# A two-layer conditioned decoder trunk on one Trainium2 core: another way through the opening, modulations on another engine, and a search over instruction orders

## The chip, the core and the metric

The kernel runs on one core of one Trainium2 chip. The core has five instruction streams that run side by side and meet only at semaphores: TensorE (PE: matmuls, transposes), VectorE (DVE), ScalarE (ACT), GpSimd (POOL) and SyncE (SP, which here issues nearly all DMA transfers). SBUF and PSUM are its on-chip memories; matmul results appear in PSUM and are read from there by DVE or ACT. The metric is the device time of one execution in microseconds (us), as the median of the runs; lower is better.

## The reference

Two layers over 256 tokens of width 1024 (batch 1). Each layer is a half-step SwiGLU FFN (width 2816), a token mixer, and another half-step FFN; layer 0 mixes with MoBA attention (16 heads of 64; with 256 tokens there is a single block, so it is causal attention with a relative bias), layer 1 with MLA attention on low-rank queries and a shared K/V. Every part starts with an RMS norm and a modulation whose shift, scale and gate come from the conditioning vector c:

```python
def rms_norm(x, g):
    return x * rsqrt(mean(x * x, -1) + EPS) * g
def modulate(h, shift, scale):
    return h * (1 + scale) + shift
def swiglu(h, w_gate, w_up, w_down):
    return (silu(h @ w_gate) * (h @ w_up)) @ w_down

c_act = silu(c)
for layer in range(2):
    mods = c_act @ ada_w[layer] + ada_b[layer]
    sh1, sc1, g1, sh2, sc2, g2, sh3, sc3, g3 = split(mods, 9)
    h = modulate(rms_norm(x, norm_g[layer, 0]), sh1, sc1)
    x = x + 0.5 * g1 * swiglu(h, ffn_w_gate[layer, 0], ffn_w_up[layer, 0], ffn_w_down[layer, 0])
    h = modulate(rms_norm(x, norm_g[layer, 1]), sh2, sc2)
    if layer == 0:
        mix = moba_attention(h, ...)
    else:
        k, v = mla_shared_kv(x, c_act, ...)   # own norm, shift and scale on x, then down and up projections
        mix = mla_attention(h, ..., k, v)
    x = x + g2 * mix
    h = modulate(rms_norm(x, norm_g[layer, 2]), sh3, sc3)
    x = x + 0.5 * g3 * swiglu(h, ffn_w_gate[layer, 1], ffn_w_up[layer, 1], ffn_w_down[layer, 1])
```

All data are float32.

## The kernel before

**Products.** A float32 product is made of three matmuls in the type fp32r: each operand is split into a rounded part "hi" and the rest "lo", and hi x hi, lo x hi and hi x lo are added in PSUM (`mm3`, lines 774 to 776). The split is made on the chip: ACT copies with rounding (`hi`, L644 for weights, L789 for activations), and DVE subtracts (`lo`, L645 and L790; `split_evac` is this pair for activations). Weights come from HBM through SP's queue into `raw` tiles, once each, as 128-row slabs of up to 1024 columns, and are used once.

**Conditioning.** The shift and scale columns of a norm (`m_cols`, one value for each of the 1024 features, laid out over partitions) are c_act times a slab of adaLN weights. `column` (L655) does 128 of them at a time: DVE multiplies a 128x1024 slab `adaw` (512 KB) with `c_b`, which holds c_act in every partition, and reduces. `scale_col` (L660) then turns the scale column s with the norm's gain g into (s + 1) g.

**Opening.** `first` (from L1518) serves the first FFN. c arrives as 32 rows of 256, is put through Silu (L1562, L1563), split (L1564), and eight matmuls (L1568) with a stationary operand `row_r` that selects one row broadcast it to all partitions; ACT copies the two PSUM tiles to `c_b` (L1571). Matmuls on zeros (L1579, "fills") keep PE at work and open the six accumulators `accs`. x is normed: the first row tile's square sum on DVE (L1589), the second's on ACT (L1586), `rstd` on POOL (L811), and a diagonal matrix with it (L1593) lets a matmul transpose and scale x at once (L1603); for later k a transpose is used (L1608). Then a loop over k = 0 to 7, one step for each 128 features: two `column` reduces, `scale_col`, the modulation `z` by ACT (L1620), its split into h (L789, L790), the split of the first FFN's weights for these features (`whi` by ACT, L1631; `wlo` by DVE, L1632; 768 KB a step, a 1024-column and a 512-column part, three 512-column parts at k = 0), and 36 matmuls (L1640 to L1642) into the six accumulators.

**Mixer entry.** After an FFN, `norm_T` norms a row tile (t = 0 or 1, 128 tokens) and `modulate_cols` (L816) treats it 256 columns at a time: ACT scales by rstd (L819), PE transposes (L824), and `modulate` (L836) applies scale and shift to each 128x128 block, by DVE (L840) or by ACT (L842), before the split. Before MLA this is done for two keys at once: the layer's own norm, (1, 1), into `h`, and the shared K/V's, "kv", into `hkv`. The line that selects the engine sends all of the second key to DVE, and of the first key the columns from 512 on. Behind it come the low-rank projections, whose results are normed and transposed into `qlT` and `ckT` (from L1397) and projected up.

**Order.** The kernel is first written down as one list of instructions. `Order` (L250) then chooses, for each of the five engines, the order in which its instructions are issued, by placing them one by one on a model of the chip with a cost for each (`duration`, L203) and a time by which it is needed (`needs`, L362); `place` (L377) does one placement, `work_out` (L517) repeats it four times with the PE times of the last one and keeps the best, and `apply` (L531) pins that order. Within an engine instructions run strictly in this order, and an instruction that waits holds up all behind it. `place` adds a cost when PE turns to plain float32 matmuls (`SWITCH`).

Of the kernel before, what the change touches and what calls it, by code (L numbers as in the profile page):

```python
# [4 lines left out]

# [16 lines left out]
P = 128  # L22
D = 1024
KD = D // P
S = 256
# [157 lines left out]

WAKE = 100.0
SWITCH = 95.0
COLD = 5600.0
TABLE = 1280.0
RATE = 330.0
# [4 lines left out]
MARGIN = 400.0  # L193
GATE_MARGIN = 3000.0
ROUND_OF_ORDER = 4
ENGINES = ("PE", "DVE", "Activation", "Pool", "SP")


# [4 lines left out]
def duration(i, aps):  # L203

    kind, e = type(i).__name__, i.engine.name
    n = max([elements(x) for x in aps] or [0])
    if kind == "InstDMACopy":
        return (700.0 if e == "Pool" else 330.0), 0.0
    if e == "PE":
        if kind != "InstMatmult":  # L210
            return 12.0, 12.0
        cols, dt = elements(aps[-1]), i.ins[0].dtype
        if i.is_transpose:
            c = 109.0
        elif dt == F32R:
            c = max(256, cols) / 2.4 + 13.3
        elif dt == F32:
            c = 2 * max(112.0, cols / 1.2 + 2.5)
            if DH in (aps[-1].ap[0][1], aps[0].ap[0][1]):
                c /= 2  # L220
        else:
            c = max(29.0, cols / 2.4 + 7.0)
        return c, c + 165.0
    psum = any(x.tensor.space == PSUM for x in aps)
    if e == "DVE":
        if kind == "InstTensorScalarPtr":
            full = len([x for x in aps if elements(x) == n]) > 2
            d = 205.0 + (1.05 if full else 0.54) * n if n > 8 else 155.0
            if aps[-1].tensor.dtype == mybir.dt.bfloat16 and n > 8:
                d = 267.0 + 0.42 * n  # L230
        elif kind == "InstTensorCopy":
            d = 150.0 + (1.045 if psum else 0.53) * n
        elif kind == "InstMemset":
            d = 60.0 + 0.84 * n
        else:
            d = 155.0 + 1.09 * n if kind in ("InstISA", "InstCustomDveAnt") else 150.0 + 1.045 * n
        return max(d - 83.0, 40.0), d
    if e == "Activation":
        d = (165.0 if psum else 195.0) + 0.845 * n + 95.0 * (len(aps) - 2) + 15.0 * (len(i.outs) > 1)
        return d - 110.0, d  # L240
    if e == "Pool":
        if kind == "InstTensorTensor":
            d = 600.0 + 300.0 * n if n <= 8 else 150.0 + 4.5 * n
        else:
            d = 60.0 + 0.9 * n if kind == "InstMemset" else 140.0 + 1.22 * n
        return d - 70.0, d
    return 50.0, 50.0


class Order:  # L250
# [4 lines left out]
    def __init__(self, nc, tc, rank, held, late, anchor):  # L255
# [34 lines left out]
        for name, us in self.uses.items():  # L290
            t = self.tiles[name]
            if t.space == DRAM:
                continue
            tag = str(t.tag).rsplit("_", 1)[0]
            pool = max((p for p in pools if tag.endswith("_" + p)), key=len)
            r = self.ring[name] = pool, tag
            if r not in self.bufs:
                self.bufs[r] = pools[pool].tag_meta[tag[:-len(pool) - 1]].bufs
            l = self.rings.setdefault(r, [])
            if l and self.uses[l[-1]][0] != us[0]:  # L300
                self.after[self.uses[l[-1]][0]].append(us[0])
                self.npre[us[0]] += 1
            if len(l) >= self.bufs[r]:
                self.next_tile[l[-self.bufs[r]]] = name
            l.append(name)
            for u in us:
                self.tiles_of[u].append(name)

    def add(self, i, seen, masks):
# [67 lines left out]
    def place(self, need):  # L377
# [68 lines left out]
        while placed < n:  # L446
# [68 lines left out]
        return order, max(done)  # L515

    def work_out(self):  # L517
        t, pe_time, best = 0.0, [0.0] * len(self.ins), None
        for k, e in enumerate(self.eng):
            if e == "PE":  # L520
                pe_time[k] = t
                t += self.cost[k][0]
        for _ in range(ROUND_OF_ORDER):
            order, end = self.place(self.needs(pe_time))
            if best is None or end < best[0]:
                best = end, order, self.start, self.done
            pe_time = self.start
        self.best = best
        return best

# [8 lines left out]
def trunk(ctx: ExitStack, tc: tile.TileContext, a: dict, out: bass.AP):  # L539
# [276 lines left out]
    def modulate_cols(t, r, keys, c0, n, wait):  # L816
# [4 lines left out]
        def fin():  # L821
            pt = tr_tile()[:, :n]
            for j in range(n // P):
                nc.tensor.transpose(kslice(pt, j), kslice(y, j), ident)  # L824
            pe(n // P * 0.11)
            for i, (key, h) in enumerate(keys):
                z = tp.tile([P, n], F32, tag="y", name=nm("z"), bufs=4) if i else y
                step = n if c0 or i else P
                for c in range(0, n, step):
                    modulate(pt[:, c:c + step], z[:, c:c + step], key, (c0 + c) // P, step,  # L830
                             on_vector=i > 0 or len(keys) > 1 and c0 >= 512)
                    split_h(h, c0 + c, step, z[:, c:c + step])
        due[0] = max(clock[0] + wait, due[0] + 0.01)
        later(due[0] - clock[0], fin)

    def modulate(xT, z, key, k0, n, on_vector=False):  # L836
        for j in range(n // P):
            shift, scale = [col_slice(i, key, k0 + j, 1) for i in range(2)]
            if on_vector:
                nc.vector.tensor_scalar(kslice(z, j), kslice(xT, j), scale, shift, op0=ALU.mult, op1=ALU.add)  # L840
            else:
                nc.scalar.activation(kslice(z, j), kslice(xT, j), AF.Identity,  # L842
                        scale=scale, bias=shift)

    def split_h(h, c0, n, z):
        ks = slice(c0 // P, (c0 + n) // P)
# [43 lines left out]
    def kslice(tile_, k):  # L890
        return tile_[:, k * P:(k + 1) * P]
# [626 lines left out]
    def first(units):  # L1518
# [5 lines left out]
        with ExitStack() as st:  # L1524
# [2 lines left out]
            with ranked(0):  # L1527
                nc.vector.memset(zeros, 0.0)

            c4, chi, clo = [tp.tile([P, S], x, tag="y", name=nm("c"), bufs=4)[:32] for x in (F32, F32R, F32R)]  # L1530
            row_r = fp.tile([32, 4], F32R, name="row_r")
            nc.vector.tensor_copy(row_r, ident[:32, :4])
            wt = [[splitp.tile([P, D], F32, tag=g, name=nm("adaw")) for g in ("hi", "lo")] for _ in range(KD)]
            cuts = (0, FIRST_A, n1)
            raws = [rawp.tile([P, 2048], F32, tag="raw", name=nm("raw")) for _ in range(3)]
# [10 lines left out]
                        nc.sync.dma_start(w[:, c1:c1 + step], src[:, c1:c1 + step])  # L1546

            with ranked(0):
                nc.scalar.dma_start(c4, a["c"])
                nc.scalar.dma_start(all_cols, a["cols"])  # L1550
            for t in range(NT):
                with ranked(t):
# [6 lines left out]
                    with ranked(2 * k + 3):  # L1559
                        load_w(k)  # L1560
            with ranked(0):
                nc.scalar.activation(chi, c4, AF.Silu)  # L1562
                nc.scalar.activation(c4, c4, AF.Silu)  # L1563
                nc.vector.tensor_tensor(clo, c4, chi.bitcast(F32), op=ALU.subtract)  # L1564
                pc = [tr_tile() for _ in range(2)]
                for x in (chi, clo):
                    for k in range(4):
                        nc.tensor.matmul(pc[k // 2][:, k % 2 * S:(k % 2 + 1) * S], row_r[:, k:k + 1].to_broadcast([32, P]), x,  # L1568
                                         start=x is chi and k % 2 == 0, stop=x is clo and k % 2 == 1)
                for i in range(2):  # L1570
                    nc.scalar.activation(c_b[:, i * 512:(i + 1) * 512], pc[i], AF.Copy)  # L1571
            hold(lambda: nc.scalar.activation(cact, cact, AF.Silu), 10e3)
            ps_x = [tr_tile(), ps_ada.tile([P, 512], F32, tag="ada", name=nm("tr"))]
            accs = [tr_tile() if f >= 4 else mm_tile() for f in range(B1)]


            for f in range(B1):
                for i in range(2 if 1 <= f < 4 else 1):
                    nc.tensor.matmul(accs[f], zeros, zeros[:, None].to_broadcast([P, 4, P]), start=i == 0, stop=False)  # L1579
            diag, rs, y, fill = [], [], {}, 10  # L1580
            for t in range(NT):
# [32 lines left out]
            for k in range(KD):  # L1614
                with ranked(2 * k + 2):
                    for i in range(2):
                        column(key, i, k, wt[k][i])
                    scale_col(key, k, 1)
                    z = tp.tile([P, S], F32, tag="y", name=nm("z"), bufs=4)
                    nc.scalar.activation(z, xT[k], AF.Identity, scale=col_slice(1, key, k, 1), bias=col_slice(0, key, k, 1))  # L1620
# [73 lines left out]
```

## Time and profile before

| | |
|---|---|
| median of 3 runs | 994.26 us (993.56 to 994.35) |
| the profiled execution: its own time | 993.19 us |
| the profiled execution: its span | 990.8 us |
| PE busy | 979.4 us, 5565 matmuls |
| DVE busy | 845.8 us |
| ACT busy | 629.2 us |
| POOL busy | 85.6 us |
| moved by DMA | 260.55 MB, 263 GB/s in the mean |

The span runs from the first to the last instruction of the profile; the execution's own time has a little more around it. The stages lie one behind the other: opening and first FFN to about 200 us, MoBA to about 330, two FFNs to 690, MLA's entry to 730, the rest of MLA to 830, the last FFN to the end.

A row of the timeline reads: start in us, duration in us, engine, line of the kernel, operation, what is written from what, shape, how many in a row; in brackets the time that the engine sat idle before it, and what released it. Rows with a count are several instructions merged, and their duration covers all of them. Neighbouring rows of one engine overlap a little, since an instruction's start lies ahead of the end of the one before. A row of the list of waits gives the waiting line and what it waited for, then the total in us, how many times, and the longest.

### The profile page before, as it was taken

To read this page: it belongs to the slowest core of one execution; us is meant where nothing else is said; L and a number is where in the kernel's file an instruction comes from. 1 tells how busy PE (TensorE), PEld (TensorE's weight loads), DVE (VectorE), ACT (ScalarE), POOL (GpSimd) and SP (SyncE) were. 2 spreads that over 40 slices of the span, in tenths; PEclk is the share of its full clock that TensorE was granted. 3 is DMA by queue.
4 is the path that set the end of the run, shared out by engine and by line. 5 is a ranking of instruction groups with operands and counts; after the bars stand their busy time and mean duration, and the time that the engine had idled before them with its cause. 6 is when DMAs were issued, how large, how long until landed. Compare 5 with 4: busy or idle time off the path is not lost.

```text
span 990.8 us, 15241 instructions
## 1 busy us (share of the span) xinstructions
PE 979.4 (99%) x5565; PEld 832.1 (84%) x5565; DVE 845.8 (85%) x1431; ACT 629.2 (64%) x1176; POOL 85.6 (9%) x120
## 2 busy tenths in 40 slices
PE   8999999999999999999999999999999999999998
PEld 7988888888887788888888888888888878888886
DVE  7999999898999899999798999974899789677542
ACT  5699565378666966555377665633869796666421
POOL 1012100022131000000010000000143110000000
PEclk9999999999999999999999999999999999999999
DMA  9978989898777678989889988872333568545630
GB/s 367 409 268 280 348 304 370 290 362 304 270 282 259 240 291 317 324 305 347 299 312 323 329 315 335 286 287 88 107 112 128 213 241 300 182 170 175 228 128 21
DMA packets 53274, 260.55 MB, mean 263 GB/s; under 512 B 6192, under 2 KB 6736, under 8 KB 35024
## 3 DMA queue, kind: packets, MB, share of 16 engines
q1 hardware_dynamic: 51696, 255.93, 70.8%
q0 software_dynamic: 1024, 3.17, 1.1%
q8 instruction: 43, 0.70, 0.3%
q10 hardware_dynamic: 480, 0.49, 0.2%
q14 instruction: 31, 0.25, 0.1%
HBM read 255.37 MB, written 4.19 MB: 262 GB/s over the span
## 4 chain that ended last, share of the span: by engine, by line
PE 93%; DVE 3%; DMA 2%; ACT 1%; issue 1%; POOL 0%; ACTq 0%; SPq 0%
PE mm L979 26%; PE mm L774 15%; PE mm L775 15%; PE mm L776 15%; PE mm L987 13%; DMA raw<-in_first_dram 2%; PE at L1103 1%; PE at L1083 1%; PE at L1043 1%; PE tr L1204 1%; PE tr L824 1%; PE tr L1475 1%; PE at L1048 1%; DVE wlo L1632 1%; DVE adaw L655 1%
## 5 line engine op out<-in xcount | busy, mean ns | idle before, releaser
L645 DVE TENSOR_TENSOR lo<-raw,hi 128x1024 fp32r<-128x1024 f32 (+3 forms) x312 | 369.7, 1200 | 69.2 <-ACT hi L644 63.7
L644 ACT ACTIVATE hi<-raw 128x1024 fp32r<-128x1024 f32 (+3 forms) x312 | 320.8, 1038 | 152.5 <-PE mm L776 115.9
L979 PE MATMUL mm<-h,hi 128*128 128x512 f32 x1120 | 288.6, 394 | 0.0
L979 PEld LDWEIGHTS mm<-h,hi 128*128 128x128 f32 x1120 | 199.6, 189 | 34.4
L987 PEld LDWEIGHTS mm<-h,lo 128*128 128x128 f32 x1120 | 155.5, 190 | 12.1
L987 PE MATMUL mm<-h,lo 128*128 128x256 f32 x1120 | 162.3, 283 | 0.0
L655 DVE CUSTOM_DVE_ANT_0 adaw<-adaw,c_b,cols 128x1024 f32<-128x1024 f32 x112 | 141.5, 1278 | 3.0 <-ACT c_b L1571 1.8
L774 PE MATMUL mm<-hi,gh 128*128 128x512 f32 x352 | 137.5, 390 | 0.0
L775 PE MATMUL mm<-lo,gh 128*128 128x512 f32 x352 | 137.2, 390 | 0.0
L776 PE MATMUL mm<-hi,gl 128*128 128x512 f32 x352 | 137.2, 390 | 0.0
L774 PE MATMUL mm<-hi,h 128*128 128x512 f32 (+1 forms) x240 | 95.2, 401 | 0.4 <-ACT h L789 0.3
L776 PE MATMUL mm<-hi,h 128*128 128x512 f32 (+1 forms) x240 | 92.6, 392 | 1.0 <-DVE h L790 1.0
L775 PE MATMUL mm<-lo,h 128*128 128x512 f32 (+1 forms) x240 | 93.0, 391 | 0.0
L776 PEld LDWEIGHTS mm<-hi,gl 128*128 128x128 f32 x352 | 66.1, 188 | 13.9
L775 PEld LDWEIGHTS mm<-lo,gh 128*128 128x128 f32 x352 | 66.1, 188 | 13.3
L774 PEld LDWEIGHTS mm<-hi,gh 128*128 128x128 f32 x352 | 66.1, 188 | 13.3
L693 DVE SCALAR_TENSOR_TENSOR acc<-adaw,cols,acc 128x1024 f32<-128x1024 f32 x48 | 61.3, 1278 | 0.2
L774 PEld LDWEIGHTS mm<-hi,h 128*128 128x128 f32 x240 | 45.1, 188 | 10.2 <-issue 1.3
L776 PEld LDWEIGHTS mm<-hi,h 128*128 128x128 f32 x240 | 45.1, 188 | 10.1 <-DVE h L790 1.2
L775 PEld LDWEIGHTS mm<-lo,h 128*128 128x128 f32 x240 | 45.2, 188 | 7.8
L811 POOL TENSOR_TENSOR rstd<-ssq,mhalf 128x1 f32<-128x1 f32 x12 | 13.5, 1125 | 411.0 <-DVE ssq L806 344.0
L916 ACT ACTIVATE u<-mm 128x256 f32<-128x256 f32 x70 | 26.4, 377 | 34.8 <-PE mm L987 33.6
(240 smaller groups left out, 1246.7 us busy)
## 6 DMA issues: line engine op xcount, KB each, us to landing
raw<-in_w_dram SPq DMA_DIRECT2D x142, 1024.0 KB, 5.4
adaw<-in_ada_dram SPq DMA_DIRECT2D x160, 512.0 KB, 5.5
raw<-in_w_dram SPq DMA_DIRECT2D x12, 512.0 KB, 3.5
raw<-in_first_dram SPq DMA_DIRECT2D x7, 512.0 KB, 9.0
raw<-in_w_dram SPq DMA_DIRECT2D x6, 576.0 KB, 3.7
bias_d<-bt SPq DMA_DIRECT2D x12, 256.0 KB, 3.9
bg<-bias_d POOLq DMA_DIRECT2D x4, 768.0 KB, 6.2
raw<-in_first_dram SPq DMA_DIRECT2D x10, 256.0 KB, 9.0
```

The lines of the kernel that those rows point to most:

```text
L644: nc.scalar.activation(hi, src, AF.Copy)
L645: nc.vector.tensor_tensor(lo, src, hi.bitcast(F32), op=ALU.subtract)
L655: nc.vector.tensor_tensor_reduce(wt, wt, c_b, 1.0, cols[:, i, c:c + 1], op0=ALU.mult, op1=ALU.add, accum_out=m_cols[:, i, c:c + 1])
L693: nc.vector.scalar_tensor_tensor(acc, ada_tile(j, k), cact[:, k:k + 1], acc, op0=ALU.mult, op1=ALU.add)
L774: nc.tensor.matmul(ps, lh, rh, start=start, stop=False)
L775: nc.tensor.matmul(ps, lh, rl, start=False, stop=False)
L776: nc.tensor.matmul(ps, ll, rh, start=False, stop=stop)
L811: nc.gpsimd.tensor_tensor(r, stats[t], mhalf[:, 0:1], op=ALU.pow)
L824: nc.tensor.transpose(kslice(pt, j), kslice(y, j), ident)
L916: nc.scalar.activation(x, ps[:, S:], AF.Copy)
L979: nc.tensor.matmul(ps[i], w[0], hs[2], start=k == 0, stop=False)
L987: nc.tensor.matmul(ps[i][:, S:], w, hk_, start=False, stop=k == KD - 1)
```

## The change

There are four parts.

1. In the opening, the c tiles `chi` and `clo` take all 128 partitions instead of 32: c fills rows 0 to 31 and DVE memsets clear the others, and `row_r` becomes 128x4. c's DMA is issued ahead of the others. The second half of `c_b` is copied by DVE. Accumulators 1 to 3 get four fills each instead of two. In each of the eight steps the scale column is made by ACT (Identity with scale g and bias g) instead of DVE. At k = 0, ACT writes the rounded h straight from PSUM, DVE makes z from PSUM as well, and the difference is lo.
2. In the mixer entry with two keys, the first key's columns from 512 on go to DVE only for t = 0; for t = 1 (four 128x128 blocks) ACT does them. `modulate` takes the block width as an argument, since the opening now uses it with 256.
3. The planner's model: turning from plain float32 matmuls to others costs `BACK`, going from a transpose to a product saves 80 ns, a DVE operation with two column operands has a cost of its own, an instruction on a newer tile of a ring of buffers isn't placed ahead of the first use of the one before it, and the broadcast matmuls of c are kept in one group.
4. `work_out` goes on with 400 trials: it picks one of the waits of PE in the planned schedule, weighted by length, disturbs the need times of the other engines' instructions before it at random, places everything again, and keeps the result if the planned end falls by more than 1 ns.

```diff
+BACK = 140.0
+T_TO_R = -80.0
+TRIALS = 400
...
+            elif len(aps) > 3 and not full:
+                d = 267.0 + 1.05 * n if n > 8 else d
...
             if l and self.uses[l[-1]][0] != us[0]:
-                self.after[self.uses[l[-1]][0]].append(us[0])
-                self.npre[us[0]] += 1
+                for u in us:
+                    if u != self.uses[l[-1]][0]:
+                        self.after[self.uses[l[-1]][0]].append(u)
+                        self.npre[u] += 1
...
-            half = type(i).__name__ == "InstMatmult" and aps[0].ap[0][1] == DH
+            half = type(i).__name__ == "InstMatmult" and (aps[0].ap[0][1] == DH or aps[1].ap[-1][0] == 0)
...
-                slow = self.ins[k].ins[0].dtype == F32 and not self.ins[k].is_transpose
-                if slow and not dtype:
-                    occ, dur = occ + SWITCH, dur + SWITCH
-                dtype = slow
+                kind = ("transpose" if self.ins[k].is_transpose else
+                        "slow" if self.ins[k].ins[0].dtype == F32 else "product")
+                d = (SWITCH if kind == "slow" and dtype != "slow" else 0.0 if kind == "slow" else
+                     BACK if dtype == "slow" else
+                     T_TO_R if dtype == "transpose" and kind == "product" else 0.0)
+                occ, dur = occ + d, dur + d
+                dtype = kind
...
         for _ in range(ROUND_OF_ORDER):
-            order, end = self.place(self.needs(pe_time))
+            need = self.needs(pe_time)
+            order, end = self.place(need)
             if best is None or end < best[0]:
-                best = end, order, self.start, self.done
+                best, kept = (end, order, self.start, self.done), need
             pe_time = self.start
+        rnd = random.Random(12)
+        for _ in range(TRIALS):
+            _, order, start, _ = best
+            pe = order["PE"]
+            waits = [(start[b] - start[a] - self.cost[a][0], start[b]) for a, b in zip(pe, pe[1:])]
+            waits = [w for w in waits if w[0] > 80.0]
+            at = rnd.choices([t for _, t in waits], [w for w, _ in waits])[0]
+            back, by = 15e3 * rnd.choice((0.3, 1, 2)), 1e3 * rnd.choice((0.3, 1, 3))
+            need = [x + rnd.gauss(0, by) if e != "PE" and at - back <= t < at + 300.0 else x
+                    for x, t, e in zip(kept, start, self.eng)]
+            order, end = self.place(need)
+            if end < best[0] - 1.0:
+                best, kept = (end, order, self.start, self.done), need
...
-                    modulate(pt[:, c:c + step], z[:, c:c + step], key, (c0 + c) // P, step,
-                             on_vector=i > 0 or len(keys) > 1 and c0 >= 512)
+                    modulate(pt[:, c:c + step], z[:, c:c + step], key, (c0 + c) // P, P,
+                             on_vector=i > 0 or len(keys) > 1 and t == 0 and c0 >= 512)
...
-            c4, chi, clo = [tp.tile([P, S], x, tag="y", name=nm("c"), bufs=4)[:32] for x in (F32, F32R, F32R)]
-            row_r = fp.tile([32, 4], F32R, name="row_r")
-            nc.vector.tensor_copy(row_r, ident[:32, :4])
+            c4, chi, clo = [tp.tile([P, S], x, tag="y", name=nm("c"), bufs=4) for x in (F32, F32R, F32R)]
+            with ranked(0):
+                nc.scalar.dma_start(c4[:32], a["c"])
+                for x in (chi, clo):
+                    for p in (32, 64):
+                        nc.vector.memset(x[p:2 * p].bitcast(F32), 0.0)
+            row_r = fp.tile([P, 4], F32R, name="row_r")
+            nc.vector.tensor_copy(row_r, ident[:, :4])
...
-                        nc.tensor.matmul(pc[k // 2][:, k % 2 * S:(k % 2 + 1) * S], row_r[:, k:k + 1].to_broadcast([32, P]), x,
+                        nc.tensor.matmul(pc[k // 2][:, k % 2 * S:(k % 2 + 1) * S], row_r[:, k:k + 1].to_broadcast([P, P]), x,
                                          start=x is chi and k % 2 == 0, stop=x is clo and k % 2 == 1)
-                for i in range(2):
-                    nc.scalar.activation(c_b[:, i * 512:(i + 1) * 512], pc[i], AF.Copy)
+                nc.scalar.activation(c_b[:, :512], pc[0], AF.Copy)
+                nc.vector.tensor_copy(c_b[:, 512:], pc[1])
...
-                for i in range(2 if 1 <= f < 4 else 1):
+                for i in range(4 if 1 <= f < 4 else 1):
                     nc.tensor.matmul(accs[f], zeros, zeros[:, None].to_broadcast([P, 4, P]), start=i == 0, stop=False)
...
-                    scale_col(key, k, 1)
+                    g = col_slice(2, key, k, 1)
+                    nc.scalar.activation(col_slice(1, key, k, 1), col_slice(1, key, k, 1), AF.Identity, scale=g, bias=g)
                     z = tp.tile([P, S], F32, tag="y", name=nm("z"), bufs=4)
-                    nc.scalar.activation(z, xT[k], AF.Identity, scale=col_slice(1, key, k, 1), bias=col_slice(0, key, k, 1))
                     hh, hl = [h0[0][3][:, k, i].rearrange("p t q -> p (t q)") for i in range(2)]
-                    split_evac(hh, hl, z)
+                    if k:
+                        modulate(xT[k], z, key, k, S)
+                        split_evac(hh, hl, z)
+                    else:
+                        modulate(xT[k], hh, key, k, S)
+                        modulate(xT[k], z, key, k, S, on_vector=True)
+                        nc.vector.tensor_tensor(hl, z, hh.bitcast(F32), op=ALU.subtract)
```

Here `nc.scalar` is ACT, `nc.vector` DVE and `nc.tensor` PE; `ranked` gives instructions an early need time; P is 128, S 256, KD 8.

More of the change, by code (lines that the diff above doesn't have):

```diff
@@ L3 @@
 import math
+import random
 from contextlib import ExitStack, contextmanager
@@ L836, in modulate @@
     def modulate(xT, z, key, k0, n, on_vector=False):
-        for j in range(n // P):
+        for j in range(xT.shape[-1] // n):
+            js = slice(j * n, (j + 1) * n)
             shift, scale = [col_slice(i, key, k0 + j, 1) for i in range(2)]
             if on_vector:
-                nc.vector.tensor_scalar(kslice(z, j), kslice(xT, j), scale, shift, op0=ALU.mult, op1=ALU.add)
+                nc.vector.tensor_scalar(z[:, js], xT[:, js], scale, shift, op0=ALU.mult, op1=ALU.add)
             else:
-                nc.scalar.activation(kslice(z, j), kslice(xT, j), AF.Identity,
-                        scale=scale, bias=shift)
+                nc.scalar.activation(z[:, js], xT[:, js], AF.Identity, scale=scale, bias=shift)
     def split_h(h, c0, n, z):
@@ L1548, in first @@
             with ranked(0):
-                nc.scalar.dma_start(c4, a["c"])
                 nc.scalar.dma_start(all_cols, a["cols"])
@@ L1561, in first @@
             with ranked(0):
-                nc.scalar.activation(chi, c4, AF.Silu)
-                nc.scalar.activation(c4, c4, AF.Silu)
-                nc.vector.tensor_tensor(clo, c4, chi.bitcast(F32), op=ALU.subtract)
+                nc.scalar.activation(chi[:32], c4[:32], AF.Silu)
+                nc.scalar.activation(c4[:32], c4[:32], AF.Silu)
+                nc.vector.tensor_tensor(clo[:32], c4[:32], chi.bitcast(F32)[:32], op=ALU.subtract)
                 pc = [tr_tile() for _ in range(2)]
```

## The prediction

> **What bounds the kernel now.** I read first the page's totals and its chain of waits, then the table of stretches, then the list of what TensorE (PE) waited for, and last the timeline of each engine at the two places that the change touches.
>
> ```profile
> span 990.8 us, 15241 instructions
> PE 979.4 (99%) x5565; PEld 832.1 (84%) x5565; DVE 845.8 (85%) x1431; ACT 629.2 (64%) x1176; POOL 85.6 (9%) x120
> PE 93%; DVE 3%; DMA 2%; ACT 1%; issue 1%; POOL 0%; ACTq 0%; SPq 0%
> ```
>
> PE is busy for 979.4 of 990.8 us and holds 93% of the chain that ended last. So nothing can be won but PE's own holes, 11.4 us in all by this view, and the table of stretches says where they are (columns: stretch, its length, then PE, PE's weight loads, DVE, ACT and POOL busy with their counts, the granted clock, DMA share, GB/s):
>
> ```profile
> 0.00:12.20 12.20, 9.48 (x35) 5.77 (x36) 6.21 (x15) 6.86 (x15) 3.93 (x26) 1.00 0.86 327
> 12.20:50.00 37.80, 37.37 (x302) 35.98 (x300) 36.73 (x68) 24.66 (x42) 0.00 (x0) 1.00 1.03 408
> ...
> 200.00:330.00 130.00, 129.62 (x717) 104.60 (x716) 119.77 (x229) 95.69 (x198) 29.00 (x17) 1.00 0.79 287
> 330.00:690.00 360.00, 360.00 (x1872) 307.93 (x1871) 321.92 (x468) 214.10 (x357) 7.51 (x7) 1.00 0.82 299
> 690.00:730.00 40.00, 37.04 (x207) 32.25 (x205) 36.54 (x99) 29.01 (x75) 11.60 (x10) 1.00 0.36 116
> 730.00:830.00 100.00, 99.90 (x606) 83.56 (x605) 87.04 (x161) 82.99 (x191) 18.61 (x17) 1.00 0.53 193
> ```
>
> Idle PE: 2.72 us before the first product (0 to 12.2), 0.43 in the rest of the opening, 0.38 in MoBA, none in the FFN between 330 and 690, 2.96 in MLA's entry (690 to 730), 0.10 in the rest of MLA. In the opening's second stretch DVE is busy for 36.73 of 37.80 us and the DMA engines are full; in MLA's entry DVE is busy for 36.54 of 40 us.
>
> ```profile
> PE tr L1603 <- ACT diag L1593: 1.5, 1, 1.5
> ...
> PE mm L776 <- DVE h L790: 1.0, 1, 1.0
> PE mm L774 <- ACT ckT L789: 0.8, 1, 0.8
> PE mm L774 <- ACT qlT L789: 0.6, 1, 0.6
> PE mm L776 <- DVE qlT L790: 0.3, 1, 0.3
> ```
>
> The first is in the opening, the other four (2.7 us) are MLA's entry. What one of these costs is a little more than its idle time, because the matmul behind it starts without overlap.
>
> **The change part by part.** Everything is counted in the profiled execution, 993.19 us with a span of 990.8.
>
> (1) Up to the first product. The rows that set it:
>
> ```profile
> 4.44 0.41 DVE L1564 TENSOR_TENSOR c<-c,c 32x256 fp32r<-32x256 f32 x1 [2.14 <-ACT c L1563]
> 6.61 1.08 ACT L1571 ACTIVATE c_b<-tr 128x512 f32<-128x512 f32 x2 [2.20 <-PE tr L1568]
> 7.80 1.28 DVE L655 CUSTOM_DVE_ANT_0 adaw<-adaw,c_b,cols 128x1024 f32<-128x1024 f32 x1 [1.80 <-ACT c_b L1571]
> 10.99 0.56 ACT L1620 ACTIVATE z<-tr,m_cols 128x256 f32<-128x256 f32 x1 [0.45 <-PE tr L1603]
> 11.59 0.42 ACT L789 ACTIVATE h<-z 128x256 fp32r<-128x256 f32 x1
> 12.21 0.78 PE L1640 MATMUL mm<-h,whi 128*128 128x256 f32 x2
> ```
>
> The four memsets that clear rows 32 to 127 of the two c tiles fall into DVE's 2.14 us before L1564; without that cover they would cost, by the 128x128 memset below (0.17 us), up to twice that each for 256 columns, 1.4 us. The six added fills take 3.17/7 = 0.45 us each, 2.7 us:
>
> ```profile
> 0.93 0.17 DVE L619 MEMSET ones_r<- 128x128 f32 x1
> 1.00 3.17 PE L1579 MATMUL mm<-zeros 128*128 128x512 bf16 x7 [1.00 <-DVE zeros L1528]
> ```
>
> They lie in PE's waits for c and for the diagonals (1.5 us, and the 2.72 of the first stretch less its 1.00 at the start), and the changed order has eight fills before c's products and seven behind them; PE is late for nothing there. Splitting c_b's copies between ACT and DVE frees ACT 0.54 us earlier (half of 1.08), so the second half of x gets its square, its rstd and its diagonal some 0.8 us sooner. The columns start hardly sooner, since the first adaLN weights arrive only then (SP's issue and the landing time of such transfers):
>
> ```profile
> 1.65 0.90 SPq L1557 DMA_DIRECT2D adaw<-in_ada_dram  x2
> DMA to landing us min/median/max: 6.0/9.0/10.4
> ```
>
> 1.65 + 6.0 = 7.65, so the two reduces end near 10.15 instead of 10.3. From there the changed kernel has one pass of ACT (hh straight out of PSUM, 0.56 us) where the old one had z, a column copy and h (10.99 to 12.01): the first product starts near 10.95 instead of 12.21. A lead of 1.25 us.
>
> (2) From there to 50 us. The last step as the old kernel runs it:
>
> ```profile
> 37.61 1.28 DVE L655 CUSTOM_DVE_ANT_0 adaw<-adaw,c_b,cols 128x1024 f32<-128x1024 f32 x1
> 42.20 1.28 DVE L655 CUSTOM_DVE_ANT_0 adaw<-adaw,c_b,cols 128x1024 f32<-128x1024 f32 x1
> 44.62 0.15 DVE L660 SCALAR_TENSOR_TENSOR m_cols<-m_cols,cols 128x1 f32<-128x1 f32 x1
> 44.69 1.22 DVE L1632 TENSOR_TENSOR wlo<-raw,whi 128x1024 fp32r<-128x1024 f32 x1
> 46.23 0.68 DVE L1632 TENSOR_TENSOR wlo<-raw,whi 128x512 fp32r<-128x512 f32 x1
> 38.51 1.58 ACT L1631 ACTIVATE whi<-raw 128x1024 fp32r<-128x1024 f32 x2 [1.88 <-DMA raw<-in_first_dram]
> 43.05 1.59 ACT L1631 ACTIVATE whi<-raw 128x1024 fp32r<-128x1024 f32 x2 [1.82 <-DMA raw<-in_first_dram]
> 44.80 0.56 ACT L1620 ACTIVATE z<-tr,m_cols 128x256 f32<-128x256 f32 x1 [0.16 <-DVE m_cols L660]
> 45.40 0.42 ACT L789 ACTIVATE h<-z 128x256 fp32r<-128x256 f32 x1
> 45.87 0.74 PE L1640 MATMUL mm<-h,whi 128*128 128x256 f32 x4
> ```
>
> DVE needs 4.59 us for a step (37.61 to 42.20), the weights land every 4.54 us (38.51 to 43.05), and PE's last step starts at 45.87, 0.05 behind the end of h. A lead at the front can't reach the end of this: the last weights still land at 43.05. The change takes 0.07 us a step off DVE (the scale column, 44.62 to 44.69) and puts a column of 0.20 us into ACT's queue:
>
> ```profile
> 11.46 0.20 ACT L1572 ACTIVATE cols<-cols 128x8 f32<-128x8 f32 x1
> ```
>
> In the changed order of steps 2 to 4, 6 and 7, ACT does the 1024 columns of whi, the scale column, the 512 of whi, then z and h. Behind that column on ACT stand whi, z and h, and DVE's wlo and lo wait for those. The scale's reduce is the first of the two on DVE there, so it is done while ACT still splits weights. Last step: whi from 43.05, the column near 44.05, whi's second part to 44.75, z and h (0.60 + 0.42 by the rows) to 45.8 or 45.95, against 45.82. In step 5 the scale's reduce comes second and h some 0.3 late, which the later landings partly take back. I take 0.0 for the whole opening; bounds −1.25 (the lead lives on) and +3.9 (rival C).
>
> The Trainium skill, "TensorE: Matmul & The Clock Gate", section "Part 1: The HAM clock gate (the "warmup" mystery)", says that TensorE runs at half rate until it has been busy for about 3.4 us; by that, more fills could bring a warm PE to the first products. The row here goes against it as far as it can be seen, for after 10 us of mostly busy PE the ten fills at 11.18 still start 1.27/10 = 0.13 us apart or a little less, where warm 128 columns would take half (the granted clock reads 1.00 in that stretch); the sum by the page would be some 0.3 us lower up to the first products, and would be lost behind the landings like the rest of the lead.
>
> ```profile
> 11.18 1.27 PE L1610 MATMUL tr<-zeros 128*128 128x128 bf16 x10
> ```
>
> (3) MLA's entry. Four modulations of the second row tile (columns 512 to 1023 of the first key) go from DVE to ACT.
>
> ```profile
> 708.47 0.73 DVE L840 TENSOR_SCALAR y<-tr,m_cols 128x128 f32<-128x128 f32 x2 [0.27 <-PE tr L824]
> 706.88 0.79 ACT L842 ACTIVATE y<-tr,m_cols 128x128 f32<-128x128 f32 x2
> 720.54 0.48 ACT L789 ACTIVATE qlT<-tr 128x384 fp32r<-128x384 f32 x1
> 721.08 0.45 PE L774 MATMUL mm<-hi,qlT 128*128 128x384 f32 x1 [0.63 <-ACT qlT L789]
> ```
>
> One costs 0.37 on DVE and 0.40 on ACT, so DVE loses 4 x 0.37 = 1.5 us of work and ACT gains 1.6, of which its 11 idle us in this stretch take all. DVE is nearly full, so what comes behind the four on DVE (the latents' splits) comes up to 1.5 us earlier. By wait: the one of 1.0 us stays, as its modulations belong to the first row tile; that for qlT (0.6 idle, about 0.8 with the lost overlap) goes, since in the changed order the transposes stand earlier and four products are kept behind them as filler; a small one at 712 goes; the one for ckT (0.8) stays, with ACT as its source. I take −1.5, what DVE is relieved of and about half of the 2.96 us; bounds 0 and −2.9.
>
> (4) The new orders elsewhere. MoBA and the rest of MLA hold 0.38 + 0.10 us of idle PE, and the long FFN stretch none; the orders there are almost the old ones. The search accepts an order if the planner's own end falls, so it goes for these holes. I take −0.5. Bounds: −1.5 (holes too short to show as idle) and +1.0 (a hole of the size of ckT's, new).
>
> Sum: 0.0 − 1.5 − 0.5 = −2.0, so 991.2 in an execution like the profiled one. That one lies 1.07 us under the median of the runs (994.26), so I add it: 992.3.
>
> **The rivals.** B: the opening's lead survives. For it: among the ten longest waits of PE none is for a DMA, and with an earlier start the splits and SP's issues that free buffers come earlier. Against it: the whi rows wait 1.8 us for DMA in each step. It gives −2.0 − 1.25, 991.0.
>
> C, the slower side: the scale column on ACT makes each step of the opening longer. It decides where the column's reduce ends after ACT has finished the first whi, as then whi's second part, z and h stand behind it. The step is then column 0.20, whi 0.53, z 0.60, h 0.42, lo 0.34, wlo 0.60 and the two reduces 2.42, each by the distance of the rows above from what follows them, = 5.1 us instead of 4.59, and since DVE has no slack it adds up: 0.55 x 7 = 3.9. For it: step 5 has that order, and DVE is full. Against it: in the other steps the scale's reduce comes first. With parts 3 and 4 it gives +1.9, 996.2.
>
> D: the change doesn't do what it says. Only the model's waits go; those of MLA's entry come back next to where they were (ckT's for qlT's), as the new source, ACT, is 0.40 instead of 0.37 a piece. For it: three of the waits of MLA's entry end with ACT or with a split behind ACT. It gives −0.3, 993.9.
>
> **How the numbers follow.** 0.2% of 994.26 is 1.99 us, about what a measurement of this kernel can tell from no change; the bound on the fast side is 992.27. The forecast has 0.52; its own range, 990.9 to 993.7, comes from the bounds of parts 3 and 4, and the bound cuts it in halves: 0.26 faster, 0.26 same. B 0.17, all faster. C 0.16: 0.11 slower, 0.05 same (where only some steps are longer). D 0.15: 0.02 faster, 0.11 same, 0.02 slower. Together faster 0.45, same 0.42, slower 0.13. The range is 989.9 to 995.6: it holds D and most of B and leaves out C's upper half and B with all of part 3's bound.
>
> **What would show it.** In the changed profile the first product should start near 11.0, and PE's last step of the opening again within 0.3 us of 45.9 with whi landing at 43; if the last step comes near 44.7, B is right, and if it comes after 47, C. The wait for qlT from ACT should be gone from the list of waits, those for h and ckT still there, and PE's idle time between 690 and 730 near 1.5 us instead of 2.96. The prediction is wrong if the opening ends more than 0.7 us from where it did, or if MLA's entry keeps its 2.96.

## The result, and the profile after

The changed kernel takes 992.24 us (median of 15 runs, 991.36 to 993.56), the kernel before in the same runs 994.26 us (15 runs, 992.78 to 996.10). The ratio is 0.9981, with a 95% interval of 0.9974 to 0.9988: 1.9 us less, 1.2 to 2.6. That is just under the 0.2% that the prediction took for the least that can be told from no change. The forecast was 992.3.

The profiled execution tells another story: it took 993.06 us, only 0.13 less than the profiled one of before. First the page's totals and its chain of waits for the changed kernel:

```profile
span 991.2 us, 15266 instructions
PE 978.7 (99%) x5568; PEld 830.7 (84%) x5571; DVE 845.7 (85%) x1425; ACT 631.4 (64%) x1186; POOL 82.4 (8%) x120
...
PE 81%; issue 10%; DMA 4%; DVE 2%; ACT 1%; POOL 1%; SPq 0%; POOLq 0%; ACTq 0%; DVEq 0%
```

PE bounds it as before (the 10% "issue" of the chain are time in which nothing that the profile shows was waited for). To see where time goes in a kernel whose instructions are all reordered, five instructions of PE serve as milestones that every version has: the last matmul of the opening, the first down-projection product of the first FFN, that of the second FFN, the last one of the third FFN (MLA's entry follows), and the first one of the fourth. From PE's timeline of the kernel before:

```profile
50.11 0.28 PE L1642 MATMUL tr<-h,wlo 128*128 128x256 f32 x1
...
150.24 0.40 PE L774 MATMUL mm<-hi,gh 128*128 128x512 f32 x1
...
452.16 0.40 PE L774 MATMUL mm<-hi,gh 128*128 128x512 f32 x1
...
698.72 0.39 PE L776 MATMUL mm<-hi,gl 128*128 128x512 f32 x1
...
925.98 0.40 PE L774 MATMUL mm<-hi,gh 128*128 128x512 f32 x1
```

and of the changed one:

```profile
50.37 0.28 PE L1681 MATMUL tr<-h,wlo 128*128 128x256 f32 x1
...
152.14 0.40 PE L802 MATMUL mm<-hi,gh 128*128 128x512 f32 x1
...
454.84 0.40 PE L802 MATMUL mm<-hi,gh 128*128 128x512 f32 x1
...
701.42 0.39 PE L804 MATMUL mm<-hi,gl 128*128 128x512 f32 x1
...
926.44 0.40 PE L802 MATMUL mm<-hi,gh 128*128 128x512 f32 x1
```

The changed kernel is 0.26 us late at the end of the opening, 1.90 late in the first FFN, 2.7 late when MLA begins, and only 0.46 late after it. So the stretch from 699 to 926 us is 2.2 us shorter (225.02 against 227.26), and that is nearly all taken back by what lies before it in this execution. It holds MLA and the last FFN up to its down-projection, and is called MLA for short below.

What the prediction said of MLA's entry can be read from the list of PE's waits of the changed kernel between 692 and 735 us, whole, and from its busy times in the same 40 us of the work (from 692.7, as it is 2.7 us late there) and the 30 us behind:

```profile
PE mm L804 <- DVE h L818: 1.2, 1, 1.2
PE mm L802 <- ACT ckT L817: 0.5, 1, 0.5
PE mm L803 <- DVE lo L673: 0.5, 1, 0.5
```

```profile
692.70:732.70 40.00, 37.75 (x223) 34.20 (x222) 36.46 (x99) 31.91 (x82) 8.63 (x10) 1.00 0.33 102
732.70:762.70 30.00, 29.68 (x211) 25.13 (x211) 28.54 (x70) 27.43 (x72) 13.82 (x11) 1.00 0.46 150
```

The waits for h and for ckT are still there, both waits for qlT are gone, and one for a weight's lo on DVE has grown from 0.2 to 0.5. PE does 223 matmuls in these 40 us where it did 207; its idle time is 2.25 us against 2.96.

### The profile page after: what moved, and what is told of

Its sections match the earlier page's. It is cut to its first block, busy times and chain, and to the rows that moved or that the text cites. A ratio compares the mean times of both kernels' runs of the same rounds, so it can differ in the third digit from the quotient of the medians.

```text
span 991.2 us, 15266 instructions
## 1 busy us (share of the span) xinstructions
PE 978.7 (99%) x5568; PEld 830.7 (84%) x5571; DVE 845.7 (85%) x1425; ACT 631.4 (64%) x1186; POOL 82.4 (8%) x120
## 4 chain that ended last, share of the span: by engine, by line
PE 81%; issue 10%; DMA 4%; DVE 2%; ACT 1%; POOL 1%; SPq 0%; POOLq 0%; ACTq 0%; DVEq 0%
PE mm L1008 21%; PE mm L802 13%; PE mm L804 13%; PE mm L803 13%; PE mm L1016 11%; DMA raw<-in_first_dram 3%; DMA bias_d<-bt 1%; PE at L1132 1%; PE at L1112 1%; PE at L1072 1%; DVE lo L673 1%; PE tr L852 1%; PE tr L1504 1%; PE at L1077 1%; PE mm L1679 0%
```

## The experiments

All times are medians; "before" is the kernel before, run beside it on the same chip. The table at the end gives every version's stretches.

**The changed kernel again.** No edit.

> The changed kernel once more, for a second trace and a second median. Time 992.2 by both theories. The first trace has holes of PE at 117 and 122 us, behind DVE's gated products in the first FFN, which the old kernel's trace hasn't, and is 1.9 us behind the old one at 188 us. If these lie in the order, they are here again, within 0.3 us; if they were chance, this trace is less than 0.8 us behind at that point.

992.43 us against 994.23 (0.9978, 0.9969 to 0.9988). The second trace belongs to an execution of 991.59 us. It is 1.09 us late in the first FFN instead of 1.90, of which 0.86 are there at the end of the opening already; MLA is 2.28 us shorter than in the first trace of before (2.23 in the first of the changed kernel). So the gain in MLA lies in the order of instructions. For the first FFN neither branch is met in number, since the opening alone passes the bound of 0.8; but the two holes of PE are gone, and from the end of the opening to the first down-projection this trace loses 0.23 where the first lost 1.64. How much is lost there differs from execution to execution. ACT's timeline shows the difference; the first trace:

```profile
106.38 0.42 ACT L817 ACTIVATE gh<-g 128x256 fp32r<-128x256 f32 x1 [2.39 <-DMA bias_d<-bt]
```

and the second:

```profile
105.56 0.42 ACT L817 ACTIVATE gh<-g 128x256 fp32r<-128x256 f32 x1 [0.57 <-DMA bias_d<-bt]
```

ACT can't write `gh` before the last store of a bias tile to HBM has landed (the wait is put down to it). SP issues this store at 98.64 in the first trace and at 97.95 in the second:

```profile
98.64 1.02 SPq L1241 DMA_DIRECT2D bias_d<-bt  x1
```

```profile
97.95 0.84 SPq L1241 DMA_DIRECT2D bias_d<-bt  x1
```

It needs about as long in both, 7.6 and 7.4 us from issue to landing. But in the first trace it lands 0.8 us later and ACT is ready for it 1.0 us earlier, so ACT waits 1.8 us longer. DVE sits idle behind it, and then is late for PE, which had been 0.6 us ahead of the second trace up to there. In the first trace DVE's timeline and PE's have

```profile
106.83 0.43 DVE L818 TENSOR_TENSOR gl<-g,gh 128x256 fp32r<-128x256 f32 x1 [2.10 <-ACT gh L817]
```

```profile
117.62 2.57 PE L1008 MATMUL mm<-h,hi 128*128 128x512 f32 x10 [0.24 <-DVE g L946]
122.83 0.73 PE L1008 MATMUL mm<-h,hi 128*128 128x512 f32 x2 [0.32 <-DVE u L946]
```

where the second has 0.28 us of idle DVE and no such wait of PE. That ACT meets this store at all belongs to the order of the changed kernel: in the three traces of before it waits there for 0.15 us at most.

**The kernel before, twice more.** No edit.

> The kernel before once more, for a second trace. Its first trace belongs to an execution 1.1 us under its median. If an execution varies by chance in the opening and the first FFN, where DMA is full, this trace differs from the first there and by less than 0.3 us from 330 us to the end.

> The kernel before, a third trace. The first two belong to executions 1.1 and 1.6 us under its median. If that is chance, this one lies nearer 994.3, and is longer in the first 190 us by what it is longer in all; from 330 us to the end it agrees with the other two within 0.2 us.

Their executions took 992.87 and 992.85 us. The first product starts 1.2 and 1.1 us later than in the first trace (13.45 and 13.34 instead of 12.21), the opening ends 0.45 and 0.34 later, and from there on no milestone moves by more than 0.1 us. So stretches behind the opening repeat within 0.1 us, and chance lies in the opening, as expected; the third trace did not come nearer to the median. All three traces of before belong to short executions of their kernel (992.85 to 993.19, with medians of 994.23 to 995.03 in four sets of runs).

**The parts alone.** Entry only: the kernel before with

```diff
-                             on_vector=i > 0 or len(keys) > 1 and c0 >= 512)
+                             on_vector=i > 0 or len(keys) > 1 and t == 0 and c0 >= 512)
```

> The kernel before with only the four modulations moved to ACT, old planner, no trials. If the move by itself is worth what I forecast, the stretch from 699 us to the last FFN is 1.3 to 1.7 us shorter than before (with the new opening under the old planner it was 1.7 shorter), and the median near 992.8. If it needs the search, the stretch is within 0.5 us of before.

992.18 us against 994.52 (0.9980, 0.9972 to 0.9989). MLA is 1.23 us shorter, just under what was expected, and no other stretch moves by over 0.15. The waits of PE in the entry, and its busy time there (0.1 us late at that point):

```profile
PE mm L776 <- DVE h L790: 1.0, 1, 1.0
PE mm L774 <- DVE qn L1496: 0.3, 1, 0.3
...
PE mm L776 <- DVE ckT L790: 0.2, 1, 0.2
```

```profile
690.10:730.10 40.00, 38.10 (x219) 33.57 (x218) 36.04 (x97) 31.63 (x81) 10.87 (x10) 1.00 0.31 95
```

Four blocks fewer on DVE take away the waits for qlT and shrink that for ckT (one of 0.3 us for `qn` is new), with PE's idle time at 1.90 instead of 2.96 us. By the ratio this one line brings as much as the whole change (0.9980 against 0.9981 and 0.9978), though its trace ends only 1.1 us before the first of before.

Opening only: the kernel before with all of the new `first`.

> The kernel before with only the new opening, old planner, no trials. By my steps 0.0: within 0.7 us of the kernel before, with the first product about 1 us earlier and the last matmul of the opening within 0.6 us of 50.0, since the weights of the fourth and the eighth step land where they did (24.9 and 43.1). If the lead lives on, the last matmul comes near 48.8. Whatever the rest of the time does comes from orders far behind the opening.

995.94 us against 995.03 (1.0014, 1.0004 to 1.0025). The first product starts at 11.17, 1.04 us early, and the opening ends 0.29 late: the lead is lost. What this trace is longer by lies behind it, 1.1 in the first FFN, 1.4 between the two down-projections of 150 and 452 us, 0.8 in the FFNs, where the old planner gave the rest another order. So the opening came as expected, and the time did not.

Opening and entry with the old planner (all of the diff from `modulate_cols` on):

> The new opening and the new mixer entry, ordered by the old planner without trials. By my steps the opening gives 0 and the entry 1.5 us: about 992.8. If the search is what counts: within 0.5 us of the kernel before. If the lead of the opening lives on under another order: below 992.

994.71 us against 994.23 (0.9999, 0.9990 to 1.0008). MLA is 1.69 us shorter, and 3.8 us are lost before it. The median lies where it should if only the search counts, but not for that reason: MLA has its gain, and the stretches ahead of it take it back.

The planner alone (the diff up to `work_out`, old opening and entry):

> The old opening and the old mixer entry, with the planner's new costs and the 400 trials. If the gain comes as I forecast it, mostly from the four modulations in MLA's entry, this gives only the 0.5 us of part 4: about 993.8 against 994.3 of the kernel before. If the gain is the search's, whatever the parts, it gives nearly all of the 2.0 us: about 992.3.

998.27 us against 994.23 (1.0038, 1.0025 to 1.0050). Both expectations fell: it is 4 us slower, in every stretch but that from 452 to 699 us. The same with another seed,

```diff
-        rnd = random.Random(12)
+        rnd = random.Random(13)
```

> The old opening and entry with the new planner, which took 998.3, with the seed of the trials 13 for 12. If that slowness is the luck of one search, this is more than 1.5 us away from 998.3. If the old parts don't suit the new planner, it is within 1 us of it.

995.49 us against 995.03 (1.0011, 1.0002 to 1.0020). So, by the two ratios, 2.7 us of the 4 were one search's luck. The new costs on the old code without trials were not run, so what is left isn't divided between costs and search.

**One part left out.** No trials:

```diff
-TRIALS = 400
+TRIALS = 0
```

> The changed kernel with 0 trials, so new parts and new costs, but no search. By my steps the four modulations bring their 1.5 us without a search: about 992.7. If the search is what counts: about 994.3.

993.10 us against 994.23 (0.9991, 0.9982 to 1.0000). In MLA 0.2 us are left of the gain; nothing is lost in the first FFN. Neither theory is met. PE's waits show that in MLA's entry a wait for qlT is still there, and that a new one has come, for the scaling `y` on ACT:

```profile
PE mm L804 <- DVE h L818: 1.2, 1, 1.2
PE tr L852 <- ACT y L847: 1.0, 1, 1.0
...
PE mm L802 <- ACT ckT L817: 0.5, 1, 0.5
PE mm L802 <- ACT qlT L817: 0.4, 1, 0.4
```

So under the new costs and without trials the kernel with the move has hardly any gain in MLA. What the move itself does there isn't shown, as the new costs without move and trials were not run.

The entry left out (the condition on t undone, all else as changed):

> The changed kernel with the four modulations of the second row tile back on DVE (opening, costs and search as changed). In the traces the changed kernel gains 2.2 to 2.3 us on the old one between 699 us and the start of the last FFN. If the four modulations bring that, it is gone here (less than 0.7 us left in that stretch), and the median is near 994. If the search brings it, 1.5 us or more are left there, and the median stays within 0.7 us of 992.3.

991.58 us (6 runs) against 994.52 (0.9968, 0.9956 to 0.9980). MLA is 1.94 us shorter without the move, so the branch for the search is the one that holds. PE's waits between 693 and 735 us, whole:

```profile
PE mm L802 <- ACT ckT L817: 0.5, 1, 0.5
PE mm L804 <- DVE h L818: 0.4, 1, 0.4
PE mm L802 <- ACT hi L672: 0.3, 1, 0.3
PE mm L803 <- DVE lo L673: 0.2, 1, 0.2
```

The waits for qlT are gone as with the move, and the one for h, which the move leaves, is 0.4 instead of 1.0. This is the fastest of all versions, though its interval overlaps that of the changed kernel.

The opening left out (`first` as before, all else as changed):

> The new entry, the new costs and the trials on the old opening. If the parts add up, this is the changed kernel less what the opening gives, and by my steps that is 0: within 0.7 us of 992.3, with the stretch from 699 us to the last FFN 2.2 us shorter than before. If the old opening is what spoils the orders under the new planner (it was 4 us slower with the old entry), it is above 995.

994.13 us against 995.03 (0.9993, 0.9983 to 1.0004). In between: MLA 0.92 us shorter, 2.4 lost before it.

The changed kernel with the seed 13:

> The changed kernel with another seed of the trials, 13 for 12. If the search finds what the chip really has, it is within 0.7 us of the changed kernel (992.3). If the result depends on the luck of one order, it is more than 1 us away, on either side.

992.95 us against 994.52 (0.9983, 0.9974 to 0.9992), within the 0.7. Its trace is 1.71 us shorter in MLA and 0.55 longer between 150 and 452 us.

All traces by stretch, as the difference to the first trace of before in us (end of each stretch by the milestones; the last column is that at the start of the fourth FFN's down-projection; rounding can shift a value by 0.01):

| version | first product | opening, to 50 | to 150 | to 452 | to 699 | MLA, to 926 | sum |
|---|---|---|---|---|---|---|---|
| before, again | +1.24 | +0.45 | 0.0 | 0.0 | 0.0 | −0.1 | +0.35 |
| before, third | +1.13 | +0.34 | 0.0 | 0.0 | 0.0 | 0.0 | +0.33 |
| changed | −1.06 | +0.26 | +1.64 | +0.79 | 0.0 | −2.23 | +0.47 |
| changed, again | −0.90 | +0.86 | +0.23 | +0.25 | 0.0 | −2.28 | −0.93 |
| changed, seed 13 | −1.29 | 0.00 | +0.08 | +0.55 | 0.0 | −1.71 | −1.07 |
| without entry | −0.18 | +0.60 | +1.08 | −0.68 | 0.0 | −1.94 | −0.92 |
| without opening | −0.28 | +0.12 | +0.98 | +1.34 | 0.0 | −0.92 | +1.52 |
| without trials | −0.68 | +0.18 | 0.0 | +0.24 | 0.0 | −0.20 | +0.23 |
| entry only | +0.95 | +0.15 | 0.0 | 0.0 | 0.0 | −1.23 | −1.11 |
| opening only | −1.04 | +0.29 | +1.10 | +1.42 | +0.84 | −0.70 | +2.95 |
| opening and entry | −1.10 | +0.18 | +1.32 | +2.07 | +0.21 | −1.69 | +2.09 |
| planner only | −0.13 | +0.33 | +1.82 | +2.30 | 0.0 | +1.31 | +5.75 |
| planner only, seed 13 | −0.14 | +0.12 | +1.22 | +1.80 | 0.0 | −0.88 | +2.23 |

The first FFN (the column to 150) costs the reordered versions up to 1.82 us, and not by that store alone. Five versions lose 0.98 to 1.82 us there without the wait for it, and PE's waits name a weight's lo on DVE (0.4 to 0.9 us, in opening only, opening and entry, without opening, and planner only) or DVE's `g` (0.3 us, in planner only with seed 13). The old order shows none of these in its three traces, nor with the entry's line alone.

## Why the prediction was right, and where not

**The opening, 0.0: right, and for the reason given.** From the timelines of ACT, and the one row of PE that starts the last step, in the changed kernel:

```profile
9.74 0.38 ACT L1652 ACTIVATE m_cols<-m_cols,cols 128x1 f32<-128x1 f32 x1
...
10.54 0.55 ACT L872 ACTIVATE h<-tr,m_cols 128x256 fp32r<-128x256 f32 x1
...
43.20 1.07 ACT L1670 ACTIVATE whi<-raw 128x1024 fp32r<-128x1024 f32 x1 [1.71 <-DMA raw<-in_first_dram]
44.17 0.37 ACT L1652 ACTIVATE m_cols<-m_cols,cols 128x1 f32<-128x1 f32 x1
44.45 0.62 ACT L1670 ACTIVATE whi<-raw 128x512 fp32r<-128x512 f32 x1
45.06 0.56 ACT L872 ACTIVATE z<-tr,m_cols 128x256 f32<-128x256 f32 x1
45.65 0.42 ACT L817 ACTIVATE h<-z 128x256 fp32r<-128x256 f32 x1
```

```profile
11.14 1.02 PE L1679 MATMUL mm<-h,whi 128*128 128x256 f32 x4
...
46.13 0.74 PE L1679 MATMUL mm<-h,whi 128*128 128x256 f32 x4
```

The first product comes at 11.14 (forecast: near 10.95), the last weights land at 43.20 as they did at 43.05, and the last step starts at 46.13, within the 0.3 us of 45.9 that were given. The table says it for thirteen more traces: first products differ by 2.5 us, ends of the opening by 0.86, and the earliest start (−1.29) ends when the first trace of before does. Rival B fell with that. Against the mean of before's three traces (+0.26) the changed kernel's two (+0.56) are 0.3 late. One term was mis-sized: the scale column, with two column operands, takes 0.37 us on ACT, not the 0.20 of the copy that I took for it. Rival C fell as well: DVE's pace stays at 4.59 us a step (its reduces start at 37.88 and 42.47), since in six of the eight steps ACT makes the column while DVE is still in its second reduce. (Its price was added up wrongly too: 5.11 less 4.59 is 0.52 us a step, 3.6 in all and not 3.9.)

**MLA's entry, −1.5: right in place and cause for the move by itself, wrong as an account of the changed kernel.** The move alone gives −1.23 in MLA, with the waits for qlT gone, those for h and ckT left. But the changed kernel has −2.2, and keeps −1.94 with the move undone. Move and search both take the waits for qlT; the step failed where it counted the move's gain and the search's as two terms, and where it gave the search too little there. Rival D, that other waits take the place of the ones removed, fell for the changed kernel, but describes the version without trials.

The idle PE time that I wanted to see, 1.5 us, is 2.25. That is no sign of a gain elsewhere: I began by saying that nothing can be won but PE's idle time, and that was wrong. (Of the 11.4 us that I named, the stretches that I listed hold 6.6; the others lie behind 830 us, where no term of mine reaches.) For MLA as a whole, in the first trace of before and the second of the changed kernel:

```profile
698.72:925.98 227.26, 224.20 (x1318) 192.99 (x1317) 187.38 (x353) 167.09 (x357) 29.00 (x25) 1.00 0.51 183
```

```profile
700.08:925.04 224.96, 222.43 (x1317) 192.39 (x1316) 186.15 (x350) 168.18 (x361) 27.65 (x25) 1.00 0.52 185
```

The stretch is 2.3 us shorter, but idle PE falls only from 3.06 to 2.53 us. The other 1.8 us lie in time that counts as busy, for the same matmuls. In the trace of before the down-projection's products of 0.39 us start 0.23 us apart (at 150.48, 150.71, 150.94), so a delay under some 0.16 us (an estimate) shows as no idle time. Which delays went was not worked out.

**The orders elsewhere, −0.5: wrong.** Between 150 and 452 us, the stretch with MoBA in it, the changed kernel loses 0.25 to 0.79 us, and the first FFN, for which I had no term, loses 0.23 to 1.64. The step took the planner's measure for the chip's: an order is kept when the planned end falls. The planner alone, the same model and the same search on the old code, makes the kernel 4 us slower with one seed and, by the ratio, 1 with another. One wait that a fixed plan can't have right in both executions is shown, that of ACT for the bias tile's store, 0.57 us in one and 2.39 in another of the same order. Which of the model's costs are wrong stays open.

**The sum: 992.3 against 992.24, closer than its terms.** By the traces the changed kernel's executions (993.06 and 991.59) are 0.6 us shorter in the mean than the three of before (mean 992.97); the stretches, mean against mean, give 0.3 + 0.9 + 0.5 − 2.2 = −0.5. By the ratio of all runs it is 1.9. I added 1.07 us to go from the profiled execution to the median; the changed kernel's traces lie 0.8 over and 0.8 under its two medians, those of before 1.1 to 2.2 under theirs. So some 1.3 us of the measured gain come from executions of the old kernel that no trace has caught. The spans of the untraced runs bear this out: their median is 992.4 to 992.9 us in three sets of before and 990.6 us for the changed kernel beside one of them, so the gain lies inside the span, and the three traced spans of before (990.8, 991.1 and 991.1) are matched by only eight of the 78 runs in those sets. Waits for DMA in the first 190 us, which moved the changed kernel by 1.4 us between two traces, could lengthen those executions; this was only argued, and stays open. That the sum came out right is in part luck: the −0.5 for the other orders had the wrong sign, the −1.5 for MLA was too small, and the 1.07 stood for a difference that no row explains. The forecast's own range, 990.9 to 993.7, was also narrower than the bounds of parts 3 and 4 added up, 989.9 to 995.3.

## What to carry to other kernels

Before counting a lead at the front, look for the last transfer that the stretch waits for: here 2.5 us of difference at the first product were gone 38 us later. Where a planner orders all instructions, each edit redraws every order, and its parts don't add up: read an edit's worth in its own stretch, from a trace with only that edit (here one line alone gave, by the ratio, as much as all four parts), and try a second seed before a search is credited or blamed. And where executions of one kernel differ by as much as the gain, a second trace of each side tells which stretches repeat (here MLA, within 0.1 us in both kernels) and which don't.

## What the runs showed of the hardware

Half-speed matmuls at the start end sooner with the new opening. Its ten fills of 128 columns take, on PE's timeline,

```profile
10.44 0.72 PE L1643 MATMUL tr<-zeros 128*128 128x128 bf16 x10
```

against 1.27 us with the old one. It is 0.72 in all seven traces with the new opening and 1.27 in all seven with the old, with a granted clock of 1.00 in both. In the changed kernel PE is at full speed earlier than that: five fills of 512 columns start some 0.22 us apart from 5.87 on, where one alone took 0.61 in the old kernel.

```profile
5.87 1.25 PE L1612 MATMUL mm<-zeros 128*128 128x512 bf16 x5
```

```profile
5.24 0.61 PE L1579 MATMUL tr<-zeros 128*128 128x512 bf16 x1
```

The Trainium skill ("TensorE: Matmul & The Clock Gate", section "Part 1: The HAM clock gate (the "warmup" mystery)") gives about 3.4 us of sustained work as what brings PE to full speed. My reading, that the old trace speaks against it, stands for the old opening, where in the first trace PE works from 1.00 to 7.00 us without a gap and is still slow at 11.18; it doesn't hold for the new one, which starts at 0.99 and is fast by 5.87.

The two differ in the rows of c's products (32 and 128) and in the number of fills. That more fills in one piece are enough is what the trace without the entry suggests: eleven run there ahead of c's products, and the first four of these products are fast already: they take 0.73 us, where four with as many columns took 1.22 in the old kernel.

```profile
0.99 4.62 PE L1612 MATMUL mm<-zeros 128*128 128x512 bf16 x11 [0.99 <-DVE zeros L1557]
5.95 0.73 PE L1601 MATMUL tr<-c,row_r 128*128 128x256 f32 x4 [0.34 <-ACT c L1595]
```

Whether the 128 rows alone would do was not tried. Nothing of it reaches the end of the opening, as the weights' landing sets that.
